# Attention and MLP layer on one core: modulation columns by single VectorE passes, x by feature, float32 scores of two heads, output projection by input halves, eight late projection chunks

## The chip, the cores and the metric

One NeuronCore of a Trainium2 chip runs the whole kernel. The time is device microseconds for one execution; 1126.22 us is the median of three runs of the kernel before (1123.72 to 1126.37). The engines are TensorE (PE in the profile, its weight loads PEld), VectorE (DVE), ScalarE (ACT), GpSimd (POOL) and SyncE (SP), whose queue issues the weight loads. A smaller time is better.

## What is computed

```python
c_act = jax.nn.silu(c)
mod = c_act @ mod_w[i] + mod_b[i]
sh_m, sc_m, g_m, sh_f, sc_f, g_f = jnp.split(mod, 6, axis=-1)
hmix = x * (1.0 + sc_m[:, None, :]) + sh_m[:, None, :]
y = windowed_gqa_sink(hmix, positions, w_qkv, b_qkv, sink, w_o, b_o)
x = layer_norm(DEEPNORM_ALPHA * x + (1.0 + g_m[:, None, :]) * y, ln_mix_g, ln_mix_b)
hff = x * (1.0 + sc_f[:, None, :]) + sh_f[:, None, :]
y = sq_relu_mlp(hff, mlp_w1, b1, mlp_w2, b2)
x = layer_norm(DEEPNORM_ALPHA * x + (1.0 + g_f[:, None, :]) * y, ln_mlp_g, ln_mlp_b)
```

There is one layer: 256 tokens (two tiles of 128), 2048 features, 32 query heads of 64 with 8 key/value heads, rotary positions, a window of 128 and a sink logit for each head, then an MLP of width 8192. All is float32: x and the weights come from HBM in float32, and mod_w alone is 96 MB, which is multiplied with one vector only.

## The kernel before

**Streaming.** All weights come in chunks of 1 MB (128 x 2048 float32) through the class `Stream`, in the order of its list: SP's queue loads them into 5 (at first 8) raw buffers, ACT casts each half to a high part `wh` (L253), and DVE subtracts it to get a low part `wl` (L224). A product takes three TensorE instructions in fp32r (`mm3`: high by high L500, high by low L501, low by high L502), each 128 x 128 by 512, so one chunk takes 24 of them; a float32 matmul is two records in the trace. "Chunk n" below counts these main chunks.

**Modulation.** Of the 96 chunks of mod_w, 50 are multiplied on TensorE: `Mod.quad` (L313) sends the same column of c_act, repeated 32 times, to four column groups of 32 with four different pieces of the chunk. The other 46 are multiplied on VectorE, two instructions of 128 x 1024 for each chunk (L352, the first of a group L350), which add into two tiles over all chunks; another quad with ones (`g,onesf`) then sums these over the partitions. `columns` transposes the row that results into columns for scale and shift. A gate stays a row: `gate` spreads it over 128 partitions by matmuls (L397).

**The early stage, 0 to 159.7 us.** Main chunks 0 to 17 of the QKV projection, group by group of input features (`MIXG` gives the groups' sizes in blocks of 128 features). A group can start when `modulated(g)` has scaled its x (ACT L536, DVE L537 and L538), which needs all modulation chunks of that group. x comes by rows and is transposed by `turn_x` (L524). Results go from PSUM into sums in SBUF by DVE (L554).

**The attention slots, 159.7 to 382.3 us.** The two first late chunks of the projection, then a loop of 21 slots: slot n computes the scores of one head group and token tile (`scores`, L737 and L738, with q and k split in high and low parts by L694 and L695 and transposed by L705), adds the mask (L740), takes the maximum (L742), exponentials (L751), and does the transposes (L776) and the values (L791) of the slot before. Beside them each slot has one main chunk: a late projection chunk in slots 0 to 3, none in slot 4, and one chunk of the output projection in slots 5 to 20 (`project(j, c)`: the inputs in four parts j, the outputs in four parts c; each adds its result to `ys` in SBUF by DVE, L851 to L858). `SLOT_FILL` says how many modulation chunks (gate m, then the MLP's) stand ahead of each slot's chunk in the list.

**After it.** The first LayerNorm (382.3 to 391 us), where TensorE has modulation chunks to do, then the MLP. The gate of the MLP is computed by VectorE between 556 and 730 us and spread at 766 us.

Each engine takes its instructions in order; the build's scheduler has set that order by then.

## Time and profile before

| what | value |
|---|---|
| median of 3 runs | 1126.22 us (1123.72 to 1126.37) |
| the profiled execution, its span | 1125.2 us |
| TensorE busy | 1088.7 us (97%) |
| VectorE busy | 809.9 us (72%) |
| ScalarE busy | 545.2 us (48%) |
| HBM read | 285.38 MB |
| main chunks, modulation chunks | 18 early and 22 in the slots; 96 |

The span is the time from the first instruction to the last in the one execution that was profiled; the runs are timed without a profile. Matmuls are pipelined, so that one instruction's duration is longer than the distance to the next; where a cost on TensorE is wanted, the distance between two starts is read.

### The profile page before, as it was taken

The page shows a single profiled execution, that of the slowest core. Times are in us where ns is not written, and L with a number is a line of the kernel's source. Part 1 is how long each engine was busy: PE and PEld are TensorE (multiplying, and loading weights), DVE is VectorE, ACT ScalarE, POOL GpSimd, SP SyncE. Part 2 cuts the span into 40 slices and gives each one's busy share as a digit, 9 for nine tenths or more (in the row PEclk, how much of TensorE's full clock was granted, in tenths as well). Part 3 has the DMA queues.
Part 4 walks back from the last instruction along what each step waited for, and adds up shares of the span by engine and source line. Part 5 has one row for each costly group of instructions (what it writes and reads, how often), then busy time and mean ns, then how long its engine had stood idle before and what let it go on. Part 6 is the DMA issues. An engine that isn't in the chain of part 4 may idle for free.

```text
span 1125.2 us, 15752 instructions
## 1 busy us (share of the span) xinstructions
PE 1088.7 (97%) x6250; PEld 880.2 (78%) x6250; DVE 809.9 (72%) x1121; ACT 545.2 (48%) x852; POOL 21.9 (2%) x40
## 2 busy tenths in 40 slices
PE   8889999899999999999999999999999999999995
PEld 6667667466776699998888888888888888888884
DVE  5597896777899978765568889756665656665576
ACT  5333445577775464653345443436444344444340
POOL 2000000000000000000000000000000000000001
PEclk9999999989999999999999999999999999999998
DMA  9999995646886799555568879764555555557522
GB/s 374 420 419 419 421 414 197 230 182 250 318 310 254 274 378 336 195 187 187 192 232 331 297 287 317 294 257 159 185 186 193 200 200 188 188 187 262 187 75 75
DMA packets 42570, 288.50 MB, mean 256 GB/s; under 512 B 4720, under 2 KB 5360, under 8 KB 8704
## 3 DMA queue, kind: packets, MB, share of 16 engines
q1 hardware_dynamic: 39824, 279.85, 66.8%
q0 software_dynamic: 1792, 6.29, 1.9%
q10 hardware_dynamic: 880, 1.35, 0.4%
q8 instruction: 49, 0.80, 0.3%
q14 instruction: 25, 0.20, 0.0%
HBM read 285.38 MB, written 2.10 MB: 255 GB/s over the span
## 4 chain that ended last, share of the span: by engine, by line
PE 85%; DMA 8%; DVE 4%; ACT 2%; issue 0%; DVEq 0%; ACTq 0%; SPq 0%
PE pa L1044 16%; PE pa L500 15%; PE pa L502 15%; PE pa L501 15%; PE pa L1045 8%; DMA raw<-in_modm 4%; PE pm L313 3%; PE pa L1021 3%; PE pa L1020 3%; PE pa L1022 3%; DMA raw<-in_wqkv 2%; PE pa L791 2%; PE pt L776 1%; DVE wl L224 1%; ACT wh L253 1%; PE pa L737 1%
## 5 line engine op out<-in xcount | busy, mean ns | idle before, releaser
L224 DVE TENSOR_TENSOR wl<-raw,wh 128x1024 fp32r<-128x1024 f32 x332 | 403.7, 1222 | 234.6 <-ACT wh L253 233.8
L253 ACT CAST wh<-raw 128x1024 fp32r<-128x1024 f32 x332 | 347.5, 1053 | 455.7 <-PE pa L502 240.5
L500 PE MATMUL pa<-wh,g 128*128 128x512 f32 x816 | 321.4, 395 | 9.2 <-ACT g L536 3.9
L502 PE MATMUL pa<-wh,g 128*128 128x512 f32 x816 | 318.8, 392 | 0.8 <-DVE g L538 0.8
L501 PE MATMUL pa<-wl,g 128*128 128x512 f32 x816 | 319.2, 391 | 0.0
L1044 PE MATMUL pa<-g,wh 128*128 128x512 f32 x768 | 271.6, 399 | 0.0
L1045 PE MATMUL pa<-g,wl 128*128 128x256 f32 x768 | 215.7, 281 | 0.0
L500 PEld LDWEIGHTS pa<-wh,g 128*128 128x128 f32 x816 | 153.4, 188 | 50.7 <-issue 6.9
L502 PEld LDWEIGHTS pa<-wh,g 128*128 128x128 f32 x816 | 153.1, 188 | 37.8 <-issue 3.3
L501 PEld LDWEIGHTS pa<-wl,g 128*128 128x128 f32 x816 | 153.5, 188 | 32.3 <-issue 2.2
L1044 PEld LDWEIGHTS pa<-g,wh 128*128 128x128 f32 x768 | 144.3, 188 | 35.8
L1045 PEld LDWEIGHTS pa<-g,wl 128*128 128x128 f32 x768 | 145.1, 189 | 0.2
L1021 PE MATMUL pa<-g,wh 128*128 128x256 f32 x256 | 72.7, 285 | 0.4 <-DVE g L964 0.4
L1020 PE MATMUL pa<-g,wh 128*128 128x256 f32 x256 | 72.5, 286 | 0.0
L1022 PE MATMUL pa<-g,wl 128*128 128x256 f32 x256 | 72.2, 283 | 0.0
L352 DVE SCALAR_TENSOR_TENSOR g<-raw,cact,g 128x1024 f32<-128x1024 f32 x53 | 67.8, 1279 | 0.5
L313 PE MATMUL pm<-raw,cact 128*32 128x256 f32 (+2 forms) x832 | 55.2, 381 | 5.0 <-DMA raw<-in_modm 3.9
L1020 PEld LDWEIGHTS pa<-g,wh 128*128 128x128 f32 x256 | 48.7, 192 | 1.3 <-issue 0.8
L1021 PEld LDWEIGHTS pa<-g,wh 128*128 128x128 f32 x256 | 49.0, 192 | 0.9 <-DVE g L964 0.8
L1022 PEld LDWEIGHTS pa<-g,wl 128*128 128x128 f32 x256 | 49.0, 192 | 0.0
L352 DVE SCALAR_TENSOR_TENSOR g4b<-raw,cact,g4b 128x1024 f32<-128x1024 f32 x32 | 40.7, 1279 | 7.5 <-DMA raw<-in_modgf 7.4
L313 PEld LDWEIGHTS pm<-raw,cact 128*32 128x32 f32 x832 | 21.6, 109 | 27.5 <-issue 12.0
(182 smaller groups left out, 836.9 us busy)
## 6 DMA issues: line engine op xcount, KB each, us to landing
raw<-in_w SPq DMA_DIRECT2D x64, 1024.0 KB, 4.9
raw<-in_w1b SPq DMA_DIRECT2D x48, 1024.0 KB, 5.0
raw<-in_modm SPq DMA_DIRECT2D x32, 1024.0 KB, 17.0
raw<-in_modf SPq DMA_DIRECT2D x32, 1024.0 KB, 6.9
raw<-in_wqkv SPq DMA_DIRECT2D x24, 1024.0 KB, 14.9
raw<-in_modgm SPq DMA_DIRECT2D x16, 1024.0 KB, 6.5
raw<-in_wo SPq DMA_DIRECT2D x16, 1024.0 KB, 6.7
raw<-in_w1a SPq DMA_DIRECT2D x16, 1024.0 KB, 7.7
```

The lines of the kernel that those rows point to most:

```text
L224: self.pinned(nc.vector.tensor_sub(l, r, f32(self.hs[n])))
L253: self.pinned(nc.scalar.copy(h, s))
L313: i = nc.tensor.matmul(self.ps[32 * j:32 * j + 32, :w], lhsT[j] if type(lhsT) is list else lhsT, rhs[j], start=self.first, stop=stop)
L352: nc.vector.scalar_tensor_tensor(p[:, :e], s, cact[:, kt:kt + 1], p[:, :e], op0=OP.mult, op1=OP.add)
L500: nc.tensor.matmul(ps, xh, wh, start=start, stop=False)
L501: nc.tensor.matmul(ps, xh, wl, start=False, stop=False)
L502: S.prev = nc.tensor.matmul(ps, xl, wh, start=False, stop=stop).ins
L1020: nc.tensor.matmul(o, wh(w, 128), hh, start=new, stop=False)
L1021: nc.tensor.matmul(o, wh(w, 128), hl, start=False, stop=False)
L1022: nc.tensor.matmul(o, wl(w, 128), hh, start=False, stop=end)
L1044: nc.tensor.matmul(ps, wh(k, 128), hb, start=k == 0, stop=False)
L1045: nc.tensor.matmul(ps[:, :256], wl(k, 128), hb[:, :256], start=False, stop=k == NK - 1)
```

## The change

- **Modulation.** A chunk for VectorE now holds 128 output features on the partitions and all 2048 inputs along the free axis. `Col.step` multiplies it with c_act, which `spread` has put on all partitions (`cb`, by 16 matmuls at the start), and sums along the free axis in one instruction of 128 x 2048 that writes one column. 54 chunks go this way, 42 go to TensorE (mix 18, gate m 8, MLP 16). The quads that summed over partitions are gone. A group's chunks for the two engines alternate in the list.
- **Gates.** A gate is now a set of columns; `Gate.spread` turns them with one matmul, writes a row to DRAM, and loads it back on all partitions with two DMAs on ACT's queue.
- **x.** It comes by feature (`xT`), so that the 32 transposes and their copies are gone; the rows of x, needed for the first residual, come at slot 16 (2 MB on SP's queue).
- **Scores.** q and k stay float32: a slot has four float32 matmuls with 64 contracted rows in place of eight fp32r ones with 128, for two heads that stand in rows 0 to 63 and 64 to 127, into two PSUM banks. Mask and extreme value come from one DVE instruction for each head (four in a slot, with four reads of the accumulator), which writes its sum to SBUF; the exponentials read that. `split_k` and `split_q` are gone, and 40 float32 transposes replace 96.
- **Output projection.** `project(p, c)` adds two input parts in PSUM over two slots, so that half of the additions to `ys` fall away.
- **Slots.** Two chunks move from the early stage to the slots: 16 early ones, 8 late ones in slots 0 to 7, the output projection in slots 8 to 23. The heads of k and of the first q are now made before the early stage ends.

```diff
+OUT_AT = 8
+X_AT = 16
+SLOT_FILL = (2, 1, 2, 1, 2, 1, 2, 1, 1, 2, 1, 2, 1, 2, 1, 2, 2, 2, 1, 2, 1, 2, 0, 0)
...
+MIXP = (1, 1, 1, 2, 2, 2)
...
+    def spread():
+
+        for c in range(4):
+            ps = psa.tile([128, 512], F32, name="pa")
+            for k in range(4):
+                kt = 4 * c + k
+                nc.tensor.matmul(ps[:, k * 128:k * 128 + 128], cact[:, kt:kt + 1].to_broadcast([128, 128]), ident,
+                                 start=True, stop=True)
+            nc.scalar.copy(cb[:, c * 512:c * 512 + 512], ps)
...
+    class Col:
+
+        def __init__(self, chunk, dst):
+            self.chunk, self.dst = chunk, dst
+
+        def plan(self, i):
+            S.plan(a["mod"][self.chunk], self.step)
+
+        def step(self, raw):
+            S.pinned(nc.vector.tensor_tensor_reduce(out=raw, in0=raw, in1=cb, scale=1.0, scalar=0.0,
+                                                    op0=OP.mult, op1=OP.add, accum_out=self.dst))
...
+            rows = [(self.m, i) for i in range(2 * p)]
+            cols = [(Col(MODS["c" + which, n, k, 0], dst[:, n, k:k + 1]), 0)
+                    for k in range(k0 + p, k0 + nk) for n in range(2)]
+            self.set(rows, cols)
...
+        def spread(self, g):
+
+            d, b = self.col[:, 8 * self.p:], self.gb[:, 8 * self.p:]
+            nc.vector.tensor_tensor(d, d, b, op=OP.add)
+            pt = pst.tile([128, 512], F32, name="pt")
+            nc.tensor.matmul(pt[:NK, :128], self.col, ident, start=True, stop=True)
+            r = sml.tile([NK, 128], F32, name="grow", bufs=1)
+            nc.scalar.copy(r, pt[:NK, :128])
+            nc.scalar.dma_start(self.row.rearrange("o (k n) -> (o k) n", k=NK), r)
+            for h in range(2):
+                nc.scalar.dma_start(g[h], self.row[:, h * 1024:h * 1024 + 1024].partition_broadcast(128))
...
-    LATE = [(4, 3), (5, 3), (4, 4), (5, 4), (4, 5), (5, 5)]
-
-    ORDER = {2: (1, 0, 2), 3: (5, 4, 3, 0, 2, 1), 4: (1, 2, 0), 5: (0, 1, 2)}
-    CARRY = {(LATE[n], LATE[n][1]) for n in (0, 2, 4)} | {((2, 2), 5), ((3, 1), 1), ((4, 0), 0), ((1, 2), 2)}
+    LATE = [(4, 3), (5, 3), (3, 4), (4, 4), (5, 4), (3, 5), (4, 5), (5, 5)]
+
+    ORDER = {2: (1, 2, 0), 3: (0, 3, 2, 1), 4: (1, 2, 0), 5: (0, 1, 2)}
+    CARRY = {((1, 2), 2), ((2, 0), 0), ((3, 1), 1), ((4, 0), 0)}
+    CARRY |= {(x, x[1]) for x, y in zip(LATE, LATE[1:]) if x[1] == y[1]}
...
+        (nc.sync if n else nc.scalar).dma_start(xt[:, :nk * 256].rearrange("p (k t) -> p k t", k=nk),
+                                                a["xT"][:, k0:k0 + nk])
+        for k in range(nk):
+            xts[k0 + k] = xt[:, k * 256:k * 256 + 256]
+
+    def load_rows():
+
+        for c in range(4):
+            xs.append(g4())
+            nc.sync.dma_start(xs[c].rearrange("p (t n) -> p t n", t=NT), a["x"][:, :, c * 512:c * 512 + 512])
...
+        pss = [psa.tile([128, 512], F32, name="pa") for _ in range(2)]
+        for i in range(2):
+            c = (2 * rp + i) * 256 + t * 128
+            for s in range(2):
+                h = slice(64 * s, 64 * s + 64)
+                nc.tensor.matmul(pss[s][:, i * 256:i * 256 + 256], qT[j][h, c:c + 128],
+                                 kT[h, j * 256:j * 256 + 256], start=True, stop=True)
+        P = g4()
         nm = sml.tile([128, 4], F32, name="nm")
-        nc.vector.scalar_tensor_tensor(nm, mx, -1.0, nsnk[:, hs], op0=OP.mult, op1=OP.min)
+        for i in range(2):
+            for s in range(2):
+                r = 2 * s + i
+                nc.vector.tensor_tensor_reduce(
+                    out=P[:, r * 256:r * 256 + 256], in0=pss[s][:, i * 256:i * 256 + 256], in1=msk[:, t], scale=-1.0,
+                    scalar=nsnk[:, hs.start + r:hs.start + r + 1], op0=OP.add, op1=OP.min,
+                    accum_out=nm[:, r:r + 1])
         es = sml.tile([128, 4], F32, name="es")
         nc.vector.tensor_add(es, nm, snk[:, hs])
-        P = g4()
         sm = sml.tile([128, 4], F32, name="sm")
-        for r in range(4):
-            nc.scalar.activation(P[:, r * 256:r * 256 + 256], pss[r // 2][:, r % 2], AF.Exp,
-                                 bias=nm[:, r:r + 1], accum_out=sm[:, r:r + 1])
+        for i in range(2):
+            for s in range(2):
+                r = 2 * s + i
+                nc.scalar.activation(P[:, r * 256:r * 256 + 256], P[:, r * 256:r * 256 + 256], AF.Exp, scale=-1.0,
+                                     bias=nm[:, r:r + 1], accum_out=sm[:, r:r + 1])
...
     def values(n):
 
-        j, t = n // 4, n % 4 // 2
+        j, t = n // 4, n // 2 % 2
         if t == 0:
             oT[j] = g4(F32R), g4(F32R)
         oh, ol = (z[:, t * 512:t * 512 + 512] for z in oT[j])
         po = psa.tile([128, 512], F32, name="pa")
-        for kt in range(NT):
-            for s in range(2):
-                c = kt * 512 + (2 * j + s) * 64
-                nc.tensor.matmul(po[64 * s:64 * s + 64], acc[5][:, c:c + 64],
-                                 PT[n - 1 + s][:, kt * 512:kt * 512 + 512], start=kt == 0, stop=kt == 1)
+        for rp in range(2):
+            for kt in range(NT):
+                for s in range(2):
+                    c = kt * 512 + (2 * j + s) * 64
+                    nc.tensor.matmul(po[64 * s:64 * s + 64, rp * 256:rp * 256 + 256], acc[5][:, c:c + 64],
+                                     PT[n - 1 + rp][:, kt * 512 + s * 256:kt * 512 + s * 256 + 256],
+                                     start=kt == 0 and rp == 0, stop=kt == 1 and rp == 1)
...
-    def project(j, c):
-        wh, wl = S.main()
-        oh, ol = oT[j]
+    def project(p, c):
+
         pss = [psa.tile([128, 512], F32, name="pa") for _ in range(NT)]
-        last = j == 3 and c == 3
-        for t, rs in [(0, range(4)), (1, range(4))] if last else [(t, (r, r + 1)) for r in (0, 2) for t in range(NT)]:
-            for r in rs:
-                s = slice(t * 512 + r * 128, t * 512 + r * 128 + 128)
-                mm3(pss[t], oh[:, s], ol[:, s], wh(r), wl(r), r == 0, r == 3)
-            if t == 1 or last:
-                S.done(not last)
-            if last:
+        last = p == 1 and c == 3
+        ws = [S.main(), S.main()] if last else []
+        for x in range(2):
+            wh, wl = ws[x] if last else S.main()
+            oh, ol = oT[2 * p + x]
+            for r2 in (0, 2):
+                for t in range(NT):
+                    if last:
+                        break
+                    for r in (r2, r2 + 1):
+                        s = slice(t * 512 + r * 128, t * 512 + r * 128 + 128)
+                        mm3(pss[t], oh[:, s], ol[:, s], wh(r), wl(r), x + r == 0, x == 1 and r == 3)
+                if not last:
+                    S.done()
+                    if r2 == 0 or x == 0:
+                        yield
...
+            y = part(ys, t, c)
+            if p == 0:
+                nc.vector.tensor_add(y, ps, bo(c))
+            else:
+                z = part(xs, t, c)
                 nc.vector.tensor_add(y, y, ps)
-                if j == 2:
-                    z = part(xs, t, c)
-                    nc.vector.tensor_mul(y, y, g1(c))
-                    nc.vector.scalar_tensor_tensor(z, z, ALPHA, y, op0=OP.mult, op1=OP.add)
-            elif not last:
-                add_gated(ps, t, c, g1, st)
-
+                nc.vector.tensor_mul(y, y, g1(c))
+                nc.vector.scalar_tensor_tensor(z, z, ALPHA, y, op0=OP.mult, op1=OP.add)
+                nc.vector.bn_stats(st[t][:, c], z)
...
-    for n in range(21):
+    for n in range(OUT_AT + 16):
...
-        if n + 2 < len(LATE):
-            w = qkv(*LATE[n + 2])
-        elif n < 5:
-            w = iter((0, 1))
+        if n < OUT_AT:
+            w = qkv(*LATE[n])
         else:
-            if n == 5:
+            if n == OUT_AT:
+                assert all(h is raws for h in S.home[S.at:]), "an early buffer is still in use"
                 ys, bo = [g4b() for _ in range(4)], bias_all(a["bo"], [g4b(), g4b()])
-            w = project((n - 5) // 4, (n - 5) % 4)
-        S.vecs(SLOT_FILL.get(n, 0) if len(LATE) - 2 <= n < 5 else 0)
+            if n % 2 == OUT_AT % 2:
+                w = project(*divmod((n - OUT_AT) // 2, 4))
...
-        if n == 12:
-            g1 = gate(m_gm)
+        if n == 15:
+            g1 = m_gm.spread([g4(), g4()])
...
+        if n == 18:
+            project_0(3)
```

The pools' sizes differ little (the `t2` tiles have 3 buffers instead of 4). Three places show how the rows moved.

VectorE in the slots, before: a slot with mask additions (L740), maxima (L742) and a modulation chunk as two additions over the chunk (L352) on `raw_1993`.

```order
L740 TENSOR_TENSOR pa_1949<-pa_1949,msk_237 128x2x128
L352 SCALAR_TENSOR_TENSOR g4_1710<-raw_1993,cact_110,g4_1710 128x1024
L742 TENSOR_REDUCE mx_1948<-pa_1949 128x2
L759 TENSOR_TENSOR rs_1910<-sm_1867,es_1864 128x4
L740 TENSOR_TENSOR pa_1956<-pa_1956,msk_237 128x2x128
L760 RECIPROCAL rs_1910<-rs_1910 128x4
L554 TENSOR_TENSOR g4_502<-g4_502,pa_1874 128x512
L695 TENSOR_TENSOR g4_1918<-g4_1729,g4_1918 128x8x64
L742 TENSOR_REDUCE mx_1948<-pa_1956 128x2
L352 SCALAR_TENSOR_TENSOR g4_1711<-raw_1993,cact_110,g4_1711 128x1024
```

VectorE in the slots of the changed kernel, the same work of one slot: "ISA" with `raw` is the pass over a modulation chunk, "ISA" with `msk` the mask and extreme value of a head; the row of 128x1 behind each is the read of its accumulator. Two more heads and two `wl` follow.

```order
L376 ISA raw_1562,colm_117<-raw_1562,cb_113 128x2048
L376 ISA colm_117 128x1
L762 ISA g4_1809,nm_1810<-pa_1803,msk_250,nsnk_106 128x256
L762 ISA nm_1810 128x1
L762 ISA g4_1809,nm_1810<-pa_1804,msk_250,nsnk_106 128x256
```

Two mask additions, two maxima and the two additions of a chunk became four instructions of 256 columns and one of 2048, each with a short one behind it.

TensorE from one slot to the next, before: values (L791), scores (L737 and L738), and the slot's first main matmul.

```order
L791 MATMUL pa_2331<-g4_2196,g4_351 64x512
L791 MATMUL pa_2331<-g4_2282,g4_351 64x512
L737 MATMUL pa_2338<-g4_1552,g4_2034 128x256
L738 MATMUL pa_2338<-g4_1565,g4_2034 128x256
...
L737 MATMUL pa_2345<-g4_1552,g4_2034 128x256
L738 MATMUL pa_2345<-g4_1565,g4_2034 128x256
...
L500 MATMUL pa_2364<-wh_2065,g4_1940 128x512
```

TensorE at the same place in the changed kernel: values (L810), scores (L755, `pa_2089` and `pa_2090` are the two banks), and the next main matmul.

```order
L810 MATMUL pa_2079<-g4_1941,g4_359 64x256 x4
L810 MATMUL pa_2079<-g4_2034,g4_359 64x256 x4
L755 MATMUL pa_2089<-g4_1366,g4_1772 128x256
L755 MATMUL pa_2090<-g4_1366,g4_1772 128x256
...
L562 MATMUL pa_1913<-wh_1874,g4_1230 128x512
L563 MATMUL pa_1913<-wl_1929,g4_1230 128x512
```

Eight matmuls of the scores became four, which alternate between two banks; the values' four became eight of half the width.

VectorE at the LayerNorm, before: the scaling of x by rows (L830), and then the first step of the MLP's input (L962).

```order
L830 TENSOR_SCALAR g4_116<-g4_116,mv_3599,r0_3605 128x512
L825 SCALAR_TENSOR_TENSOR nmr_3640<-mv_3628,r0_3634 128x1
L830 TENSOR_SCALAR g4_318<-g4_318,mv_3599,r0_3605 128x512
L830 TENSOR_SCALAR g4_620<-g4_620,mv_3599,r0_3605 128x512
L830 TENSOR_SCALAR g4_875<-g4_875,mv_3599,r0_3605 128x512
L962 TENSOR_SCALAR g4_3691<-pt_3692,a2_3643,b2_3644 128x256
L964 TENSOR_TENSOR g4_3689<-g4_3691,g4_3689 128x256
```

VectorE there in the changed kernel: the last L830 is L850 now, and the MLP's input begins at L999.

```order
L850 TENSOR_SCALAR g4_2671<-g4_2671,mv_3378,r0_3384 128x512
L835 TENSOR_TENSOR r0_3425<-r0_3425,qq_3427 128x1
L252 TENSOR_TENSOR wl_3542<-raw_3459,wh_3540 128x1024
L845 SCALAR_TENSOR_TENSOR nmr_3431<-mv_3419,r0_3425 128x1
L252 TENSOR_TENSOR wl_3546<-raw_3459,wh_3544 128x1024
L376 ISA raw_3462,modf_115<-raw_3462,cb_113 128x2048
L376 ISA modf_115 128x1
L999 TENSOR_SCALAR g4_3487<-pt_3488,a2_3434,b2_3435 128x256
L410 TENSOR_TENSOR modf_115<-modf_115,pack_87 128x2x2
```

Two subtractions for `wl` and a modulation pass of 2048 columns now stand ahead of the MLP's input on VectorE.

## Rows read from the trace of the kernel before

**Rows 1.** The page, busy time, and the chain that ended last, by engine
```profile
PE 1088.7 (97%) x6250; PEld 880.2 (78%) x6250; DVE 809.9 (72%) x1121; ACT 545.2 (48%) x852; POOL 21.9 (2%) x40
...
PE 85%; DMA 8%; DVE 4%; ACT 2%; issue 0%; DVEq 0%; ACTq 0%; SPq 0%
```

**Rows 2.** Windows by stage: length, busy us, granted clock, DMA share, GB/s
```profile
0.00:159.70 159.70, 146.63 (x1011) 105.79 (x1012) 122.28 (x180) 67.52 (x94) 5.87 (x18) 1.00 1.00 412
159.70:382.30 222.60, 213.20 (x1226) 149.17 (x1225) 180.08 (x297) 142.65 (x332) 4.23 (x6) 0.98 0.69 253
382.30:391.00 8.70, 7.62 (x101) 3.83 (x99) 7.48 (x31) 3.18 (x7) 0.00 (x0) 1.00 0.82 311
490.00:1112.80 622.80, 622.67 (x3085) 525.26 (x3083) 414.26 (x496) 271.27 (x330) 10.11 (x15) 1.00 0.61 215
200.00:230.00 30.00, 23.12 (x112) 13.38 (x111) 18.78 (x32) 21.00 (x55) 1.25 (x2) 0.87 0.67 246
```

**Rows 3.** Waits of PE, 0 to 159.7: us in total, times, longest
```profile
PE pm L313 <- DMA raw<-in_modm: 3.9, 5, 1.4
PE pa L500 <- ACT g L536: 3.9, 3, 3.2
```

**Rows 4.** The chain that ended last, 100 to 180: start us, us, what
```profile
103.62 11.81 DMA raw<-in_wqkv
...
127.92 1.48 PE pm L313 x24
...
140.62 0.43 DVE g L538
```

**Rows 5.** Groups by line and form, 0 to 159.7: xcount, busy us, mean ns
```profile
L352 DVE SCALAR_TENSOR_TENSOR g<-raw,cact,g 128x1024 f32<-128x1024 f32 x21 | 26.9, 1280 | 0.2
...
L524 PE MATMUL pt<-ident,g 128*128 128x128 f32 x32 | 4.3, 274 | 0.0
```

**Rows 6.** Timeline of PE, 335 to 364: start us, us, what
```profile
338.07 0.64 PE L313 MATMUL pm<-g,onesf 128*32 128x256 f32 x8
...
343.17 0.39 PE L737 MATMUL pa<-g,g 128*128 128x256 f32 x1
...
344.22 0.40 PE L500 MATMUL pa<-wh,g 128*128 128x512 f32 x1
...
361.45 0.39 PE L501 MATMUL pa<-wl,g 128*128 128x512 f32 x1
361.68 0.39 PE L502 MATMUL pa<-wh,g 128*128 128x512 f32 x1
362.00 1.07 PE L313 MATMUL pm<-raw,cact 128*32 128x256 f32 x16
...
363.34 0.40 PE L501 MATMUL pa<-wl,g 128*128 128x512 f32 x1
```

**Rows 7.** Groups by line, 159.7 to 382.3
```profile
L224 DVE TENSOR_TENSOR wl<-raw,wh 128x1024 fp32r<-128x1024 f32 x43 | 52.3, 1219 | 13.0 <-ACT wh L253 12.8
...
L742 DVE TENSOR_REDUCE mx<-pa 128x2 f32<-128x512 f32 x32 | 20.7, 681 | 0.0
...
L740 DVE TENSOR_TENSOR pa<-pa,msk 128x256 f32<-128x256 f32 x32 | 13.2, 428 | 13.0 <-PE pa L738 12.7
...
L705 PE MATMUL pt<-identr,g 128*128 128x128 f32 x96 | 11.4, 252 | 6.0 <-ACT g L778 3.2 <-ACT g L707 2.8
```

**Rows 8.** Timeline, 382 to 391
```profile
387.77 1.46 DVE L830 TENSOR_SCALAR g<-g,mv,r 128x512 f32<-128x512 f32 x3
...
390.35 0.54 DVE L962 TENSOR_SCALAR g<-pt,a,b 128x256 f32<-128x256 f32 x1 [1.12 <-ACT g L956]
```

**Rows 9.** Timeline of PE at the second gate, 763 to 769.5
```profile
766.21 2.61 PE L397 MATMUL pa<-g,onesr 128*128 128x512 f32 x7
768.66 0.39 PE L1044 MATMUL pa<-g,wh 128*128 128x512 f32 x1
```

More of the change, by code (lines that the diff above doesn't have):

```diff
@@ L327, in step @@
             last = self.i == self.n
-            per = 1024 // w
-            if i == self.start:
-                if not self.whole:
-                    self.part = [g4() for _ in range(2)]
-                for n, p in enumerate(self.part):
-                    nc.gpsimd.memset(p, 0.0)
-                    nc.scalar.dma_start(p[0:1], self.bias[:, n * 1024:n * 1024 + 1024])
             for k in range(kc):
@@ L401, in groups @@
-    def groups(src, sizes, dves):
-        out, c0, k0 = [], 0, 0
-        for nk, dve in zip(sizes, dves):
-            n = 2 * nk
-            out.append((Mod([src[c0 + i] for i in range(n)], 64 * nk, dve), k0, nk))
-            c0 += n
+                else:
+                    self.quad(cact[:, kt:kt + 1].to_broadcast([128, 32]), [r[:, k, j] for j in range(4)],
+                              last and k == kc - 1)
+            if last:
+                self.r = sml.tile([128, 256], F32, name="mrow", bufs=1)
+                self.out()
@@ L884, in hybrid_kernel @@
     S.behind = True
-    for n in range(21):
+    for n in range(OUT_AT + 16):
         j, i = n // 4, n % 4
```

492 lines of the change are left out of this document (227 added, 265 removed).

## The prediction

> **What bounds the kernel now.** I read the page first: TensorE is busy 97% of the span, and 85% of the chain that ended last is TensorE's own work, 8% is DMA [rows 1]. So what the change takes from TensorE comes off the time almost one for one, where nothing else stands right behind it. The windows by stage say where that is [rows 2]. The MLP (490 to 1112.8) has TensorE at 622.67 of 622.80 us; the change hardly touches it. In the attention slots (159.7 to 382.3) TensorE is busy 213.20 of 222.60 and VectorE 180.08, so VectorE has some 40 us of air; 200 to 230 is the hole, with TensorE at 23.12 of 30 and a granted clock of 0.87. In the early stage TensorE is idle 13 of 159.70 us and DMA runs full (share 1.00, 412 GB/s): a chunk of 1.05 MB needs 2.5 us there. TensorE's waits in that stage are for modulation chunks (3.9) and for the scaled x (L536, 3.9) [rows 3]. The chain shows the hand-over: a load of a projection chunk for 11.81 us, then the last quads of the last input group at 127.92, and its scaled x complete on VectorE (L538) at 140.62 + 0.43 [rows 4]. Then three chunks of the projection follow until 159.7.
>
> **The units.** Two main matmuls start 0.23 us apart (361.45, 361.68), so a chunk's 24 take 5.55. A modulation chunk on TensorE is read from one main matmul to the second after it: 361.68 to 363.34 is 1.66, less two steps of 0.23, 1.20. A quad that sums over partitions is 0.64 [rows 6]. A transpose is 4.3/32 = 0.13 in float32 [rows 5], and the 96 in fp32r take 11.4 in all, with 6.0 of waiting besides, all of it for ACT's copies [rows 7].
>
> **Early stage.** TensorE loses two chunks (11.1), three modulation chunks (23 there before, counting gate m, 20 now: 3.6), three summing quads (1.9) and the transposes of x (4.3), and gets 16 transposes for the heads of k and q (2.1): 18.8 less. DMA loses two chunks of its list: the last modulation chunk of the last group is the 44th in place of the 46th, so 5.0 us earlier; x by rows now comes later, x by feature takes its place, the same 2 MB. The stage's end moves by 5 if only the landing counts (the 17 us from the landing, which at 412 GB/s I estimate at 122 to 123, to L538 then stay), by 18.8 if only TensorE's work counts. From 80 us on TensorE had nearly no idle time, but its work can't begin before the chunk lands: the last projection chunk should land at about 128 (48 chunks and x), and a chunk, some transposes and what TensorE is behind by then follow. I take **-11**, between the two.
>
> **VectorE's new pass.** The trace has no instruction of 128 x 2048 with a sum along the row. Nearest row: L352, with two float32 operands from SBUF, takes 1280 ns for 1024 [rows 5]; two of them are 2.56 a chunk. A single pass saves one start, so 2.3 to 2.56; with the read of the accumulator (a DVE operation on four columns takes about 0.15) 2.4 to 2.7. From above I can only bound it by doubling, 4.6 (rival 1). I take 2.5: 54 passes cost what 46 chunks with two instructions and the summing did, and VectorE's load stays as it is. For the scores a slot had two mask additions of 428 and two maxima of 681, 2.2 us [rows 7]; now four instructions on 256 columns, each like L740 (0.43) and a read of 0.06 to 0.2: 2.0 to 2.5. No change. The halved additions to `ys` take 22 operations of some 0.68 from VectorE and the splits 8 more; two chunks' `wl` add four of 1.22 [rows 7]. So VectorE's sum in the slots falls to some 165 to 172, which is less than now and hidden beside TensorE as now. If that cover is gone, an excess counts in full.
>
> The Trainium skill speaks against this part: "Vector Engine (DVE) Microarchitecture Reference", "Points that are easy to get wrong", says that an operation of the scalar-tensor-tensor shape with two sources in SBUF that aren't bf16 runs at half throughput. L352 is of that shape and shows 1.25 ns an element; the trace does not show the halving beyond that, and by the rule at its worst a pass would be 4.6 us.
>
> **Slots.** TensorE gets two chunks (+11.1). Of modulation chunks it has 14 instead of 20 (-7.2) and four summing quads fewer (-2.6). The gate's 8 wide matmuls go; the second gate's 8 took from 766.21 to 768.66, 2.45 [rows 9], and one small matmul and two transposes come: -1.9. Transposes: 96 in fp32r become 24 here; 11.4 busy, of which I take 8 off the path because ends overlap with the next matmul, against 3.2: -4.8, and of the 6.0 of waiting I take 4 away, since copies remain. Scores: before, 343.17 to 344.22, 1.05 a slot [rows 6]. A float32 pass of 256 columns is read from the modulation chunk: 16 of them in four column groups in 1.0 us, so 0.25 each if groups run beside each other. Now a slot has eight passes; two heads in different row halves beside each other make 1.0, one after the other 2.0. The records of the quads show that column groups do run beside each other; that row halves do is not in the trace. I take 1.0 and 0.2 for going in and out (a modulation chunk's neighbours stand 0.32 and 0.34 apart for 0.23 [rows 6]): +0.15 a slot, **+2.4**. The Trainium skill, "TensorEngine Tiling (Array Packing)", "Key Properties", has it that tiles run independently and that a change of mode drains TensorE; the 0.2 is such a gap, and no run here shows it for row halves. Values: the same columns in twice the matmuls, +0.5. The hole at 200 to 230 lost 6.9 us of TensorE's time and some of its clock; every slot now has a chunk, so I give back 2.5. Sum: 11.1 - 7.2 - 2.6 - 1.9 - 4.8 - 4.0 + 2.4 + 0.5 - 2.5 = **-9.0**. With VectorE in front of TensorE here and there it would be 0; with no clock lost -12.
>
> Costed at nothing: the gate's way through DRAM (a row, then two loads; the first use is three slots, some 30 us, later); x by rows at slot 16 (2 MB, 5 us of a queue whose share is 0.69; first used two slots on); the 16 matmuls of `spread` (in the time in which TensorE waits for the first weights).
>
> **LayerNorm and MLP.** Before the MLP's input, L962, VectorE was free from 389.2 on, and TensorE's first MLP product waited for ACT [rows 8]. Now two `wl` and a pass, 2.4 + 2.5, stand there; ACT's half and TensorE's modulation chunks cover some: **+1.5** (0 to 4). One more modulation chunk from here on, two summing quads fewer, the second gate: 1.2 - 1.3 - 2.2 = **-2.3**.
>
> **Sum.** -11 - 9 + 1.5 - 2.3 = -20.8: 1125.2 becomes 1104.4. The runs' median is 1.0 above the profiled span, so **1105.4**. Own range of this case: -31 (early -17, slots -12, LayerNorm 0) to -12, 1095 to 1114.
>
> **Rivals.** (1) *The pass is twice as long.* Early, VectorE without its 24 additions, two splits and two chunks' work has some 83 us; 18 passes of 4.6 make 166, more than the stage had, and it ends near 172 (+12). The slots have 13 passes and doubled scores, about 210 of 222: no gain. Then 1125.2 + 12 + 0 - 0.8 + 1 = 1137. It begins to cost at 3.3 us a pass, at 4.4 the gain is gone. For it: two float32 SBUF sources and a sum along the row at once; against: L352. (2) *Row halves don't run side by side*: 16 slots at +0.95 in place of 0.15, 12.8 more: 1118. (3) *VectorE's and ACT's order decides*, not their sums: the early end moves by 5 only, the slots gain nothing: -5 - 0 + 1.5 - 2.3, 1120. For it: L538 is on the chain now [rows 4], and VectorE's passes can't be cut into two; against: TensorE was at its limit from 80 us on. (4) *It does nothing*, because DMA paces the early stage and the slots fill with waits: 1126.
>
> **How the numbers follow.** Measurements here can tell 0.3% (3.4 us) from no change. My case 0.53 (1095 to 1114), rival 2 0.17, rival 3 0.12, rival 4 0.06, rival 1 0.12. Faster: 0.82, same 0.06, slower 0.12. From 1094 to 1125 all but rival 1, half of rival 4 and a little below are held, some 0.82; that is the range.
>
> **What would show it.** The early stage's last projection chunk ends near 149 (above 155: rival 3); a pass of 2048 at 2.4 to 2.7 us (over 3.3: rival 1); the scores of a slot from first to next main matmul 1.2 us, and two records a few ns apart (2.0: rival 2); the waits for ACT before the transposes of q nearly gone; the first MLP product 20 us earlier; TensorE still over 96% busy. A long wait of TensorE for VectorE in the slots, or for the gate's loads, would prove the sum of the slots wrong.

## The result and the profile after

The changed kernel takes 1128.14 us (median of 20 runs, 1126.12 to 1129.87), the kernel before 1126.26 (20 runs, 1123.65 to 1128.41): a ratio of 1.0018, 95% interval 1.0012 to 1.0025. That is within the 0.3% that I called no change, 22.7 us above the forecast, and outside its range. The profiled span is 1125.4 us at a mean granted clock of 0.978; before, it was 1125.2 at 0.992.

The page after, busy time and the chain by engine (they answer to [rows 1]):

```profile
PE 1067.9 (95%) x6554; PEld 883.0 (78%) x6554; DVE 786.5 (70%) x1135; ACT 526.9 (47%) x811; POOL 17.1 (2%) x34
...
PE 77%; DVE 9%; DMA 7%; ACT 4%; issue 2%; POOL 0%; DVEq 0%; ACTq 0%; POOLq 0%
```

TensorE is busy 20.8 us less than before. That is, to the tenth, what my sum took from the time, and it is chance: the sum also holds landings, waits and a clock, and the stages came out otherwise. TensorE's share fell to 95%, and the chain has 77% of TensorE where it had 85%. The work went and waits came. Windows of the changed kernel by stage, with the columns of [rows 2]; the first begins at 0, the second at the first late chunk, the third at the first chunk of mlp_w2; then four short stretches:

```profile
0.00:164.80 164.80, 136.17 (x1105) 104.46 (x1105) 120.51 (x172) 63.83 (x88) 4.96 (x16) 0.93 0.97 397
164.80:379.10 214.30, 203.12 (x1319) 150.62 (x1317) 166.18 (x331) 130.33 (x303) 2.29 (x4) 0.98 0.75 277
491.80:1113.50 621.70, 620.68 (x3075) 523.29 (x3074) 410.10 (x495) 267.23 (x323) 8.12 (x13) 1.00 0.62 217
80.00:90.00 10.00, 3.09 (x65) 2.27 (x65) 7.62 (x7) 1.44 (x3) 0.00 (x0) 0.65 1.01 423
90.00:100.00 10.00, 5.98 (x13) 4.08 (x14) 5.50 (x12) 1.85 (x4) 0.00 (x0) 0.50 1.02 428
320.00:340.00 20.00, 10.03 (x82) 6.65 (x80) 7.43 (x9) 4.56 (x7) 0.10 (x1) 0.89 0.76 311
387.70:395.00 7.30, 5.32 (x28) 5.02 (x29) 6.05 (x11) 5.53 (x9) 0.00 (x0) 0.59 1.01 428
```

Against [rows 2]: the early stage ends 5.1 us later (164.8 for 159.7; 1.1 of it is the first slot's scores, which now stand ahead of that point, so +4.0), the slots take 8.3 less (7.2 without those scores), the way from their end to the first chunk of mlp_w2 takes 112.7 in place of 108.0 (that chunk began at 490.3), +4.7, and the rest is 1.3 us shorter. The short stretches are the places where it was lost. Waits of PE there (us in total, times, longest), first from 0 to 164.8, then to 379.1, then to 491.8; the first rows answer to [rows 3]:

```profile
PE pm L336 <- DMA raw<-in_mod: 13.3, 4, 6.5
PE pa L564 <- DVE g L593: 4.9, 2, 4.0
...
PE pt L740 <- DVE g L724: 1.3, 1, 1.3
...
PE pa L564 <- DVE g L814: 9.1, 1, 9.1
...
PE pt L987 <- ACT g L848: 2.3, 1, 2.3
PE pa L1058 <- DVE g L1001: 2.0, 1, 2.0
```

**Early.** The longest of these waits is TensorE's own, for a modulation chunk of the fifth group, which stands in its order ahead of the fourth group's projection (timeline; in brackets the idle time ahead and what ended it):

```profile
87.55 1.94 PE L336 MATMUL pm<-raw,cact 128*32 128x128 f32 x32 [6.45 <-DMA raw<-in_mod]
```

Then comes VectorE. The chain around 90 us (start us, us, what; it answers to [rows 4]):

```profile
79.22 13.15 DMA raw<-in_mod
92.51 2.29 DVE raw L376
94.81 0.33 DVE g L592
95.20 0.40 DVE g L593
95.65 0.79 PE pa L564
96.44 0.43 PE pa L562
```

The fourth group's scaling (L592, L593) stands on VectorE behind the pass over a chunk that lands only at 92.5, and TensorE's projection waits for it to 95.65; its matmuls then start 0.43 apart in place of 0.23, with the granted clock at 0.50, the lower of the two levels.

**Gate and LayerNorm.** VectorE's timeline, first around L903, which the code has in slot 18, then at the LayerNorm:

```profile
337.40 0.69 DVE L903 TENSOR_TENSOR g4b<-g4b,g 128x512 f32<-128x512 f32 x1 [11.28 <-DMA g<-rowm]
338.01 1.22 DVE L252 TENSOR_TENSOR wl<-raw,wh 128x1024 fp32r<-128x1024 f32 x1
339.14 0.69 DVE L814 TENSOR_TENSOR g<-pa,g 128x512 fp32r<-128x512 f32 x1
...
384.25 1.22 DVE L252 TENSOR_TENSOR wl<-raw,wh 128x1024 fp32r<-128x1024 f32 x1
385.39 0.15 DVE L845 SCALAR_TENSOR_TENSOR nmr<-mv,r 128x1 f32<-128x1 f32 x1
385.46 1.22 DVE L252 TENSOR_TENSOR wl<-raw,wh 128x1024 fp32r<-128x1024 f32 x1
386.59 2.29 DVE L376 CUSTOM_DVE_ANT_0 raw<-raw,cb 128x2048 f32<-128x2048 f32 x1
...
388.80 0.54 DVE L999 TENSOR_SCALAR g<-pt,a,b 128x256 f32<-128x256 f32 x1
```

L903 is the first user of the gate that came through DRAM. It waits 11.28 us at the head of VectorE's order, though the slots written before it aren't done; behind it stand a `wl` and L814, the values' low part, for which TensorE waits 9.1 us. The way of the gate shows on ACT's timeline: the row goes out at 321.03, the two broadcasts at 326.06, when it has landed, and they have landed at 337.4.

```profile
321.03 0.32 ACTq L458 DMA_DIRECT2D rowm<-grow  x1
...
326.06 0.86 ACTq L460 DMA_DIRECT2D g<-rowm  x2
```

At the LayerNorm two `wl` and a pass stand ahead of the MLP's input (L999), which before stood right behind L830 and waited only for ACT [rows 8].

**What came out as priced.** Groups of VectorE, 164.8 to 379.1 (they answer to [rows 5, 7]), and one slot's scores on TensorE with the next main matmul (to [rows 6]):

```profile
L376 DVE CUSTOM_DVE_ANT_0 raw<-raw,cb 128x2048 f32<-128x2048 f32 x17 | 38.9, 2286 | 4.3 <-DMA raw<-in_mod 4.3
L762 DVE CUSTOM_DVE_ANT_0 g<-pa,msk,nsnk 128x256 f32<-128x256 f32 x64 | 27.1, 481 | 1.5 <-PE pa L755 1.5
```

```profile
259.09 1.14 PE L755 MATMUL pa<-g,g 64*128 64x256 f32 x8
260.15 0.50 PE L562 MATMUL pa<-wh,g 128*128 128x512 f32 x1
```

A pass is 2.29 us and its accumulator's read 0.08. The eight passes of a slot's scores take 1.06 us; their records come in pairs, one of each row half, that start 7 ns apart (259.089 and 259.096 us), with about 0.21 us from one pair to the next behind the first. So the two row halves do run beside each other.

### The profile page after: what moved, and what is told of

Same layout as the page of the kernel before. It is cut to its first block, busy times and chain, and to the rows that moved or that the text cites. A ratio compares the mean times of both kernels' runs of the same rounds, so it can differ in the third digit from the quotient of the medians.

```text
span 1125.4 us, 16314 instructions
## 1 busy us (share of the span) xinstructions
PE 1067.9 (95%) x6554; PEld 883.0 (78%) x6554; DVE 786.5 (70%) x1135; ACT 526.9 (47%) x811; POOL 17.1 (2%) x34
## 4 chain that ended last, share of the span: by engine, by line
PE 77%; DVE 9%; DMA 7%; ACT 4%; issue 2%; POOL 0%; DVEq 0%; ACTq 0%; POOLq 0%
PE pa L1081 16%; PE pa L564 14%; PE pa L562 14%; PE pa L563 14%; PE pa L1082 8%; DMA raw<-in_mod 5%; PE pa L1058 3%; PE pa L1059 3%; PE pa L1057 3%; DVE raw L376 2%; DVE wl L252 2%; PE pm L336 2%; DMA raw<-in_wqkv 1%; ACT wh L281 1%; ACT g L772 1%
## 5 line engine op out<-in xcount | busy, mean ns | idle before, releaser
L376 DVE CUSTOM_DVE_ANT_0 raw<-raw,cb 128x2048 f32<-128x2048 f32 x54 | 123.5, 2287 | 19.1 <-DMA raw<-in_mod 19.1
L336 PE MATMUL pm<-raw,cact 128*32 128x128 f32 (+1 forms) x1216 | 46.6, 292 | 13.7 <-DMA raw<-in_mod 13.3
L336 PEld LDWEIGHTS pm<-raw,cact 128*32 128x32 f32 x1216 | 32.0, 111 | 28.1 <-DMA raw<-in_mod 14.5
L772 ACT ACTIVATE g<-g,nm 128x256 f32<-128x256 f32 x64 | 31.8, 498 | 23.4 <-DVE nm L762 23.3
```

What stands on the lines that cost most here:

```text
L336: i = nc.tensor.matmul(self.ps[32 * j:32 * j + 32, :w], lhsT[j] if type(lhsT) is list else lhsT, rhs[j], start=self.first, stop=stop)
L376: S.pinned(nc.vector.tensor_tensor_reduce(out=raw, in0=raw, in1=cb, scale=1.0, scalar=0.0, op0=OP.mult, op1=OP.add, accum_out=self.dst))
```

## Experiments

The kernel before, run beside each experiment, had medians of 1125.2 to 1126.3. A ratio is to it; gains are also given against the changed kernel's 1128.14.

**e1_gate_pe**: both gates go to all partitions by TensorE and ACT, without DRAM.

```diff
-            pt = pst.tile([128, 512], F32, name="pt")
-            nc.tensor.matmul(pt[:NK, :128], self.col, ident, start=True, stop=True)
-            r = sml.tile([NK, 128], F32, name="grow", bufs=1)
-            nc.scalar.copy(r, pt[:NK, :128])
-            nc.scalar.dma_start(self.row.rearrange("o (k n) -> (o k) n", k=NK), r)
-            for h in range(2):
-                nc.scalar.dma_start(g[h], self.row[:, h * 1024:h * 1024 + 1024].partition_broadcast(128))
+            for c in range(4):
+                ps = psa.tile([128, 512], F32, name="pa")
+                for k in range(4):
+                    kt = 4 * c + k
+                    nc.tensor.matmul(ps[:, k * 128:k * 128 + 128], self.col[:, kt:kt + 1].to_broadcast([128, 128]),
+                                     ident, start=True, stop=True)
+                nc.scalar.copy(g[c // 2][:, (c % 2) * 512:(c % 2) * 512 + 512], ps)
```

> The changed kernel with one edit: the first and second gate are spread over the partitions by 16 small TensorE matmuls and four ScalarE copies, with no trip through DRAM. Theory (in-order waits): the product with the gate (L903) stood on VectorE in front of the values' low part (L814) and waited 11.3 us for the DRAM trip, TensorE 9.1 us, and its granted clock was 0.87 from 320 to 360. Without the trip the wait is gone, some 2 us of matmuls for each gate come: 1128.1 becomes 1114 to 1118. Rival (VectorE is full in this stretch, the wait only moves): another wait of TensorE for VectorE of 5 us or more stands within 320 to 360, and the time stays at 1124 to 1129.

Measured 1117.92 us (1117.26 to 1118.37), ratio 0.9926 [0.9912, 0.9939]: 10.2 us off the changed kernel, though TensorE has 16 small matmuls for a gate in place of one. The window of the wait is full (same columns as above), and so nearly are the slots, which end at 370.2 here:

```profile
320.00:340.00 20.00, 20.00 (x133) 15.81 (x132) 14.95 (x19) 8.45 (x12) 0.00 (x0) 1.00 0.82 300
164.80:370.20 205.40, 203.84 (x1377) 153.23 (x1379) 167.23 (x336) 133.25 (x308) 2.28 (x4) 1.00 0.78 287
```

**e6_gate_used_later**: the gate's DRAM way stays, and only L903's place on VectorE moves, by an order after a later addition (L893).

```diff
-                nc.vector.tensor_add(y, y, ps)
+                S.ev = nc.vector.tensor_add(y, y, ps).ins
...
-            nc.vector.tensor_mul(y, y, g1(c))
+            i = nc.vector.tensor_mul(y, y, g1(c))
+            tc.add_manual_dep(i.ins, S.ev.name, ORDER_ONLY, reason="later")
```

> The changed kernel with its gate through DRAM as it is, and one edit: the four VectorE products of the first half's last quarter with the gate (L903, L904) are ordered behind the next quarter's addition (L893), two slots later. If the place in VectorE's order is what cost the time, and not the trip as such, the wait of 9.1 us falls to 0 to 3 and the time to 1117 to 1121, near the run without the trip (1117.9). If the trip of 16 us is too long wherever its first use stands, the next product with the gate (L894) waits instead, and the time stays at 1124 to 1128.

Measured 1118.41 us (1117.18 to 1119.68), ratio 0.9935 [0.9918, 0.9952]. VectorE's timeline: L814 at once, L903 13 us later and without a wait.

```profile
330.55 0.68 DVE L814 TENSOR_TENSOR g<-pa,g 128x512 fp32r<-128x512 f32 x1
...
344.03 1.28 DVE L903 TENSOR_TENSOR g4b<-g4b,g 128x512 f32<-128x512 f32 x2
```

The two together: the place in VectorE's order cost 10 us, and the trip itself can lie beside other work.

**e3_two_chunks_back**: the two chunks return to the early stage; slots 6 and 7 have none.

```diff
-    LATE = [(4, 3), (5, 3), (3, 4), (4, 4), (5, 4), (3, 5), (4, 5), (5, 5)]
+    LATE = [(4, 3), (5, 3), (4, 4), (5, 4), (4, 5), (5, 5)]
...
```

> The changed kernel with one part undone: the two projection chunks that were moved to the slots are early again (18 early, 6 late ones in slots 0 to 5, no main chunk in slots 6 and 7). If the filler theory holds, TensorE's early idle time falls back towards that of the kernel before (13 us; it was 28 or more) and the early stage ends at 155 to 160 with 11 us more work in it, so the total falls by 8 to 11: 1117 to 1120. If the order on VectorE decides, the time falls only as far as the scaling of the fourth group happens to stand earlier in this order (it does: behind the pass on the 25th chunk, not the 34th), which gives the same sign; slots 6 and 7 without a chunk give some back, so 1118 to 1126. What tells them apart is the wait of TensorE for VectorE's scaling (4.0 us) and for modulation chunks (13.3 us): the order theory has the first gone and the second halved.

Measured 1128.68 us (1125.91 to 1129.56), ratio 1.0017 [1.0007, 1.0027]. Missed: the two chunks do fill some of the early waits (TensorE waits 5.9 us for modulation chunks in place of 13.3), and the slots miss them as much: chunk 20 starts at 187.3 in place of 201.6, chunk 24 at 241.5 in place of 240.3. Giving the early stage its filler back gains nothing in all.

**e2_pinned_scale**: the early passes keep their place to the end of the stage, and a group is scaled before, not beside, the last chunk of the group ahead.

```diff
-            mid.append(lambda: modulated(g + 1))
+            modulated(g + 1)
...
-    S.pin = False
```

> The changed kernel with one edit in the early stage: the modulation steps keep the order of the program, and the scaling of the next input group is written one chunk earlier, so that VectorE no longer has passes over later chunks in front of it. Theory (in-order waits): the scaling of the fourth group waited for a pass whose chunk landed at 92.5 us, though its own data were there at about 75 to 80; it starts 12 to 16 us earlier, no granted clock of 0.50 between 90 and 100, and the early stage ends 7 to 13 us earlier: 1115 to 1121. Rival (the two chunks that were moved out had filled the time in which DMA brings the next group's modulation chunks): TensorE waits as long, only later, the stage ends within 3 us of where it did: 1125 to 1129.

Measured 1125.1 us (1123.8 to 1127.21), ratio 0.9993 [0.9983, 1.0004], 3.0 off the changed kernel. Missed, in an instructive way: the last early chunk starts at 144.2 in place of 152.7, but the first late one only at 161.0 in place of 164.8. The hole moved to the first heads of q, whose rotary step (L719 to L724) is on VectorE. And among the early waits the name changed: for modulation chunks 0.2 us are left of 13.3 and for L593 0.9 of 4.9, but ACT's scaling (L591), which held TensorE for 2.2 us in the changed kernel, now holds it for 11.0 (e12 shows why). Two rows of the waits and the window 140 to 160, where VectorE is busy 19.45 us:

```profile
PE pa L562 <- ACT g L591: 11.0, 4, 3.5
PE pt L740 <- DVE g L724: 4.2, 1, 4.2
```

```profile
140.00:160.00 20.00, 15.80 (x94) 11.12 (x92) 19.45 (x23) 4.74 (x8) 0.00 (x0) 0.91 0.87 353
```

**e5_chunk_before_heads**: e2, and half of the first late chunk ahead of the first heads of q and their scores.

```diff
-    run(qkv(G - 1, 2), [lambda: qT.__setitem__(0, heads_T(qA[0]))])
+    run(qkv(G - 1, 2))
...
-        if n < 16:
+        if 0 < n < 16:
             scores(n)
...
+        if n == 0:
+            qT[0] = heads_T(qA[0])
+            scores(0)
```

> As the run with the pinned order (1125.1), with one more edit: the first half of the first late projection chunk goes ahead of the transposes of the first q and the first scores, as two whole chunks did in the kernel before. Theory: with the order mended, the chunks ended 8.5 us earlier, but TensorE then waited 4.2 us for the rotary step of q (VectorE L724) and did the transposes and a modulation chunk at half the clock, 9.2 us between the last early chunk and the first late one for some 3.2 us of work; half a chunk covers the wait: 1118 to 1121. Rival (VectorE is full there, 19.45 of 20 us between 140 and 160, so that the wait reappears a slot later): 1123 to 1126 with a wait of 3 us or more for VectorE between 160 and 185.

Measured 1120.73 us (1118.84 to 1121.64), ratio 0.9954 [0.9936, 0.9971]: 7.4 us with e2's 3.0 in it. The same window:

```profile
140.00:160.00 20.00, 20.00 (x122) 14.99 (x120) 19.41 (x25) 6.36 (x9) 0.00 (x0) 1.00 0.91 371
```

VectorE is as loaded as in e2; only what TensorE has to do meanwhile differs.

**e4_first_mlp_step**: four of TensorE's modulation chunks, not two passes, come first in the LayerNorm.

```diff
+            if which == 'f' and k0 == 8:
+                self.todo = cols[:2] + rows + cols[2:]
...
-    W1_FILL = [1, 1, 1, 0, 0, 2, 0, 3, 0, 0, 0, 0, 0, 0, 0, 0]
+    W1_FILL = [0, 0, 0, 1, 1, 2, 0, 4, 0, 0, 0, 0, 0, 0, 0, 0]
```

> The changed kernel with one edit at the LayerNorm: the modulation chunks there are all TensorE's, the passes of VectorE over later ones come after the first scaling of the MLP's input. Theory: the pass in front of L999 cost a wait of 2.0 us (L1058 for L1001) and a granted clock of 0.59 from 387.7 to 395, together some 5 us: 1122 to 1125. Rival (the wait is for ScalarE and the clock falls for TensorE's idle time before): 1126 to 1129, the clock after the first MLP product still under 0.7.

Measured 1126.5 us (1125.05 to 1128.5), ratio 1.0004 [0.9994, 1.0014]. Missed. The pass is out of VectorE's way and the wait stays: two `wl` still stand ahead of the scale (`nmr`) that ACT needs.

```profile
PE pt L991 <- ACT g L852: 3.9, 1, 3.9
```

**e7_scale_before_low_parts**: e4, with the `wl` ordered after the scale.

```diff
+            if self.after:
+                tc.add_manual_dep(i.ins, self.after, ORDER_ONLY, reason="after")
...
-            nc.vector.scalar_tensor_tensor(nm, mv[:, 0:1], -1.0, rstd, op0=OP.mult, op1=OP.mult)
+            S.after = nc.vector.scalar_tensor_tensor(nm, mv[:, 0:1], -1.0, rstd, op0=OP.mult, op1=OP.mult).ins.name
```

> As the run with TensorE's chunks at the LayerNorm (1126.5), with one more edit: VectorE makes the second token tile's shift (the row nmr) before the low parts (wl) of the MLP's first chunk. In that run two wl of 1.22 us stood in front of it, and TensorE waited 3.9 us for ScalarE's scaling that needs it, with a clock of 0.50 and 0.67 behind. Theory: the wait falls to about 1.5, the clock stays near 1.00, the first MLP product comes 2 us earlier and the next 5 us run at full speed: 1121 to 1124. Rival (the chain of small operations of the LayerNorm itself is the limit, and the low parts are then late for the third product): 1125 to 1128.

Measured 1124.98 us (1122.32 to 1126.81), ratio 0.9988 [0.9978, 0.9999], 3.2 off the changed kernel and a us short of what was expected. The wait fell to 1.6 us as expected, but the granted clock stayed as low behind it (0.78 from 390 to 400, 0.82 in the changed kernel), so that half of the theory missed:

```profile
390.00:400.00 10.00, 10.00 (x70) 10.00 (x70) 8.03 (x13) 6.87 (x10) 0.00 (x0) 0.78 0.96 366
```

**e8_all_mended**: e1, e5 and e7 in one kernel.

> All mended places together: the gate by TensorE, the pinned order with the scaling one chunk earlier, half a chunk ahead of the first q's transposes, and the LayerNorm's order. If the waits are independent, the gains add: 1128.1 - 10 - 3 - 5 - 4 = 1106, and the sum of the prediction (1105.4) is then the time of this kernel's work without the four waits. If they share their cause (VectorE's total load), less than two thirds of it: above 1112.

Measured 1109.28 us (1108.62 to 1109.99), ratio 0.9854 [0.9838, 0.987]: 18.9 us off the changed kernel, where the single gains are 10.2 + 7.4 + 3.2 = 20.8. So the three are separate losses that nearly add. The largest wait of PE that is left:

```profile
PE pa L569 <- ACT g L598: 9.1, 4, 3.8
```

**e9_fill_the_gap**: e8 with eight unused 128x512 matmuls in the LayerNorm's gap (added work that the reference doesn't need).

```diff
+    ps = psa.tile([128, 512], F32, name="pa")
+    for _ in range(8):
+        i = nc.tensor.matmul(ps, identr, identr[:, None, :].to_broadcast([128, 4, 128]), start=True, stop=True)
```

> As the run with all places mended (1109.3), with 8 matmuls of 128 x 512 on constants added at the LayerNorm that compute nothing that is used (6 of them, 1.4 us, behind the modulation chunks, where TensorE waits for ScalarE). Theory (the granted clock falls after TensorE's idle time, and its price is paid behind the wait): with the gap filled the clock from 370 to 390 rises from 0.91 to 0.98 or more, and 1 to 2 us come off though work was added: 1107 to 1109. Rival (the clock falls for another reason than the gap): the clock stays near 0.9 and the time rises by 0.5 to 2: 1109.5 to 1111.

Measured 1110.21 us (1109.57 to 1111.48), ratio 0.9862 [0.9843, 0.9882]. The clock came back as the theory had it, the time didn't. The window 370 to 380, e8 first and then e9:

```profile
370.00:380.00 10.00, 9.40 (x63) 9.05 (x64) 8.49 (x15) 8.20 (x13) 0.00 (x0) 0.83 0.99 397
370.00:380.00 10.00, 9.27 (x72) 8.79 (x72) 9.56 (x15) 7.68 (x12) 0.00 (x0) 1.00 1.02 421
```

PE's timeline behind the gap, e8 first:

```profile
372.44 0.42 PE L1068 MATMUL pa<-g,wh 128*128 128x256 f32 x1
372.66 0.42 PE L1069 MATMUL pa<-g,wl 128*128 128x256 f32 x1
```

and e9:

```profile
371.69 0.28 PE L1072 MATMUL pa<-g,wh 128*128 128x256 f32 x1
371.81 0.28 PE L1071 MATMUL pa<-g,wh 128*128 128x256 f32 x1
```

0.22 and 0.12 us from start to start. But the first MLP product begins at 370.3 in place of 369.3, and the first chunk of mlp_w2 at 472.9 in both.

**e10_fifth_group_earlier**: e8, with the fifth group scaled one chunk sooner.

```diff
-        if g < G - 1 and at == len(ORDER[g]) - 1:
+        if g < G - 1 and at == len(ORDER[g]) - (2 if g == 3 else 1):
+            if g == 3:
+                while S.at < 34:
+                    S.vecs(1) if S.q[S.at][1] else S.pump(0, len(S.hs) + 1)
```

> As the run with all places mended (1109.3), with one more edit: the scaling of the fifth input group (the one that TensorE waited for at 110 us) is written one chunk earlier too, so that VectorE does it before the passes on the 37th and 39th chunk. Theory: the wait of 9.1 us for ScalarE's scaling falls to 3 to 5, chunk 10 starts at 98 to 104 in place of 110, and since VectorE is full from 140 to 160, only half of it arrives at the end: 1104 to 1108. Rival (DMA's last chunks at 128 and VectorE's load set the end of the stage): under 1.5 us gained, 1108 to 1110.

Measured 1108.25 us (1106.95 to 1109.08), ratio 0.984 [0.9823, 0.9857], the fastest complete kernel here. Chunk 10 starts at 103.4 in place of 110.2, chunk 12 at 126.9 in place of 127.6: nearly all of it is waited for again before chunk 12, now for low parts (`wl`) on VectorE:

```profile
PE pa L570 <- DVE wl L252: 6.4, 4, 3.7
```

The longest of the four, 3.7 us at 123.2, is for the second low part of chunk 11. Its cast was done by 110.5, but on VectorE it stands behind a modulation pass that begins at 119.75. The interval of e10 overlaps that of e8, so the last us is not sure.

**e11_brief_passes**: the changed kernel with VectorE's early passes cut to 256 of 2048 inputs; the other inputs' part of those columns is left out.

```diff
+            w = 256 if S.brief else 2048
-            S.pinned(nc.vector.tensor_tensor_reduce(out=raw, in0=raw, in1=cb, scale=1.0, scalar=0.0,
+            S.pinned(nc.vector.tensor_tensor_reduce(out=raw[:, :w], in0=raw[:, :w], in1=cb[:, :w], scale=1.0, scalar=0.0,
...
```

> The changed kernel, but each of VectorE's modulation passes of the early stage covers 256 of the 2048 inputs (the other inputs' part of those columns is left out), so that the 18 passes take some 0.4 us in place of 2.29: VectorE gets some 33 us free before 160 us, while the loads, TensorE's work and the slots stay as they are. Theory (what a group's scaling waits for is the landing of its last chunks): the wait at 91 to 95.6 falls by the pass alone, 1.9 us, and the rotary step's gap by a little, so 1122 to 1127. Rival (VectorE's time in passes sets the end of the early stage): the first late chunk comes 8 to 14 us earlier, at 151 to 157, and the time is 1114 to 1120.

Measured 1124.41 us (1122.68 to 1125.74), ratio 0.9991 [0.9979, 1.0003]. The first late chunk starts at 162.9, 1.9 us earlier, as the theory had it.

**e12_brief_passes_mended**: the same cut in e8.

> The same cut of the early passes in the kernel with all mends (1109.3), where TensorE still waits 9.1 us for ACT's scaling of x (L598) and VectorE is busy 19 of 20 us at the end of the stage. Theory (landing of the group's last chunks): those waits stay within 2 us of 9.1 and the time is 1107 to 1109.5. Rival (VectorE's passes): the waits fall under 4 us and the time to 1101 to 1104, which is what the forecast of -11 for the early stage would have wanted.

Measured 1107.77 us (1106.58 to 1108.92), ratio 0.9847 [0.9827, 0.9868]: 1.5 off e8. Waits of PE before 165, and the window 100 to 120:

```profile
PE pa L571 <- ACT g L600: 9.3, 4, 3.3
```

```profile
100.00:120.00 20.00, 16.68 (x176) 12.50 (x175) 10.17 (x25) 4.22 (x7) 0.00 (x0) 0.91 1.01 426
```

VectorE is busy half of the window and the wait is that of e8 (9.1), so it is not VectorE's passes that TensorE waits for. The time is the theory's, but its reason, that the group's own last chunks land so late, is not what the timelines of VectorE and ACT show:

```profile
101.60 0.15 DVE L419 TENSOR_TENSOR modm<-modm,pack 128x4 f32<-128x4 f32 x1
...
108.48 1.04 ACT L285 CAST wh<-raw 128x1024 fp32r<-128x1024 f32 x1 [8.49 <-DMA raw<-in_wqkv]
109.43 2.07 ACT L600 ACTIVATE g<-g,modm 128x256 fp32r<-128x256 f32 x4
```

The fifth group's columns are complete at 101.75. But in ACT's order its scaling (L600) stands behind the cast of chunk 11, for whose landing ACT sits idle for 8.49 us, and TensorE needs chunk 11 only at 119.7. The fourth group is held in the same way: its columns are complete at 67.4, and L600 follows at 76.65 on the cast of chunk 7 (75.69), which TensorE needs at 86.7. TensorE waits 3.3 us at each of the two, 6.7 of the 9.3. So the larger part of what is left is order again, this time ACT's. e10 fits: with the fifth group's scaling ahead of that cast, chunk 10 starts 6.8 us earlier.

## Why the prediction was wrong

**Most sizes of the work were right, the sum of waits wasn't.** The pass (2.4 to 2.7 forecast; 2.29 + 0.08), the way in and out of the scores and the two banks side by side held; rivals 1 and 2 fell with them. By the half throughput of the Trainium skill, "Vector Engine (DVE) Microarchitecture Reference", "Points that are easy to get wrong", my estimate of a pass was 4.6; the trace disagrees, with 2.29 us or 1.12 ns an element. The Trainium skill, "TensorEngine Tiling (Array Packing)", "Key Properties", says that tiles operate independently; the trace agrees, with the pairs of passes that start 7 ns apart.

**"Costed at nothing: the gate's way through DRAM ... some 30 us later"** is the step that failed most clearly. VectorE came to its first use 5 us after the row went out, 11 us before the gate had landed, and in front of work that TensorE needed: a wait of 9.1 us and a slower clock behind it, 10 us in all (e1, e6). My text took "first use" from the slot where the code needs it; the order of VectorE's instructions, in which L903 stands ahead of L814, decides it. The prediction's own last sign, a long wait of TensorE for VectorE in the slots or for the gate's loads, is what came.

**Early stage, -11: measured +4.** I chose between a lower bound of 5, set by landings, and TensorE's 18.8. The step that failed is that both bounds count only landings or TensorE's work and put the order on the engines at nothing. Three such losses stood against it. The scaling of a group stood behind a pass whose chunk belongs to a later group, and on TensorE a modulation chunk of a later group stood ahead of the projection (e2). The rotary step lay open, since the first heads of q now come with no late chunk between (e2's miss, e5). And with both mended and the passes cut to an eighth, the scaling still stands on ACT behind the cast of a chunk that isn't needed yet (e12). The last early chunk ended at about 160; above 155 was the prediction's own sign for rival 3. In e10 chunk 20 starts at 192.9, 8.7 us before the changed kernel's, which turns the +4.0 into -4.7. That is near the lower bound of 5, but it doesn't show that landings set it, since waits by order are left in e10 too. A reading was also wrong: L538 at 140.62 + 0.43 is the first of the last group's four; its scaled x was complete only at 144.4. (24 steps of 0.23 are 5.5, not 5.55; nothing hangs on it.)

**Slots, -9: measured -7 with the gate's wait in it.** Without it (e1: the first MLP product 9.0 us earlier) it is -16: TensorE is busy 203.84 of 205.40 us there. The term was mis-sized the other way. From each of its matmuls' starts to the next start, the values took 19.3 us before and 15.0 in e1 (+0.5 forecast), and the scores 18.9, now 16.0 and the first slot's 1.1 ahead of that point (+2.4 forecast). Why the values became cheaper is not shown. So the total of e8, 3.9 us from the forecast, is in part two errors that cancel.

**LayerNorm, +1.5: measured +4.7** up to the first chunk of mlp_w2, its modulation work included. The queue of two `wl` and a pass was seen, and priced as VectorE's time alone; the matmuls behind it ran at a clock of 0.59 until 395. e7 gives 3.2 back, by shorter waits and not by the clock.

**The rivals.** Rival 3, that the order on VectorE and ACT decides, named the mechanism of most of these losses, and I gave it 0.12 and a time of 1120, since I let it cancel gains and not add a new wait. Rival 4's time, 1126, is nearest, but its reason is wrong: the change did what it says, and 18.9 us of it can be had back. Its DMA half, that landings pace the early stage, is not shown.

Not settled: how much of each early loss is the wait and how much the clock behind it (e9 touches only the LayerNorm), and how far the early stage would fall, and where landings would then hold it, if the scalings stood ahead of the casts on ACT and the low parts ahead of the passes on VectorE.

## What to carry to other kernels

When a change takes work off the busiest engine, price the order on the other engines as carefully as the work: for each instruction that now waits for something new, list what stands behind it in its engine's order and who waits for that. The trip through DRAM cost nothing that shows where its first user stood late enough in its own engine's order (e6), and 10 us where it was late only in the code. And when a wait has been mended, look what the engine waits for next: here the same group's scaling was held on VectorE first and on ACT after that, each time by a chunk that it did not need.

## What was not expected of the hardware

- A 16x128 row to DRAM and back to 128 partitions took 16.4 us: 5.0 from its issue (321.03) to the issue of the two broadcasts that wait for it (326.06), and 11.3 until those (512 KB each) had landed (337.4), with DMA at a share of 0.85 in the latter stretch.
- The pass with a sum along the row ran at 1.12 ns an element for two float32 operands from SBUF, faster than the 1.25 of the two-operand instruction before it [rows 5].
- A wait can cost more than its length: behind the hole at 80 to 90 us TensorE ran at a granted clock of 0.50 to 100 us, behind the LayerNorm's at 0.59. Keeping TensorE at work with unused matmuls brought it from 0.83 to 1.00 between 370 and 380 us (e9), and gained no time.
